# A transformer layer with pooling mixer, mLSTM and experts: column sums of the modulation by row products and a DRAM turn, router logits with the weights stationary, one channel order, output projection in one run

## The chip, the cores and the metric

The kernel runs on one core of a Trainium2 chip. The metric is the device time of one execution in microseconds (us). Before the change three runs gave 1613.83, 1614.59 and 1615.7 us; the median is 1614.59 us. The engines are TensorE (PE, with its weight loads shown apart as PEld), VectorE (DVE), ScalarE (ACT), GpSimd (POOL) and SyncE (SP), which here issues nearly all loads from DRAM.

## The reference, cut to what matters

256 latent tokens and 256 context tokens, model width 2048, all float32, one layer.

```python
sh1, sc1, g1, sh2, sc2, g2 = split(silu(c) @ w_mod + b_mod, 6)       # w_mod (2048, 12288)
xn  = rmsnorm(x) * norm1_g * (1 + sc1) + sh1
u   = xn @ w_in                                                      # columns p | q | o | k | v | gates
h_m = bidirectional chunkwise mLSTM(q, k, v, gates), started from the context's k, v, gates
p   = pooling mixer(u_p);  m = head_norm(h_m) * sigmoid(u_o)
h   = x + g1 * (concat(p, m) @ w_out)                                # w_out (2048, 2048)
fn  = rmsnorm(h) * norm2_g * (1 + sc2) + sh2
logits = fn @ w_group (4 groups), fn @ w_router (32 experts)         # top-1 group, top-2 experts in it
y   = sum over chosen experts e of weight_e * ((silu(fn @ w1[e]) * (fn @ w3[e])) @ w2[e])
out = rmsnorm(h + g2 * y) * final_g                                  # w1, w3 (32, 2048, 512), w2 (32, 512, 2048)
```

## The kernel before

**Plan and stages.** The first part of the kernel (everything up to the router) follows one list of steps, `plan`, that is built at lines 164 to 256 and emitted in order at lines 1019 to 1021. Each engine executes its own instructions in the order in which they were emitted. The list has six stages: 0 to 2 work on the first 8 row blocks of `w_in` for k and v, stage 3 on the rest of k and v and all of q, stage 4 on o, p, the pooling mixer (`pool`, 16 steps) and the output projection's parts 0 and 1, stage 5 (after `join`) on part 2 and the routes. A main step of stage 3 to 5 is a group of 12 matmuls 128x512 (`mm3`: high and low halves of a float32 split, three products for each of four row blocks). Each block of weights is loaded by SP, split into `hi` on ACT (line 548) and `lo` on DVE (line 549), one job ahead of its matmuls. Other steps are spread evenly among the main ones by the weights of `weight`: `da`, `df`, and `side`.

**Modulation sums.** Channel 2 is the gate g1, 3 the shift, 4 the scale, 5 the gate g2. For each of the four, 16 steps `da` each load one [128, 2048] slice of `w_mod` (1 MB) and add it, times a column of silu(c), into a tile (`do_da`, line 513, DVE). The sum over the 128 partitions is then made by `do_df` (line 515) in four steps per channel. Channels 2 and 5 need it as a row on all partitions: one matmul 128x512 with ones. Channels 3 and 4 need it as columns: eight matmuls per step with one moving column each (line 522 in the order 128j+p, line 523 in the order 16p+j), into `A2`, `B2` for the router and `A2p`, `B2p` for the experts.

**The mLSTM** is a generator (`mlstm`, line 710): each `side` step emits it up to its next `yield`. Its PE work is small; each of its steps waits for ACT or DVE work of the step before. In stage 4 there are 50 places for such steps.

**Output projection.** `do_out` (line 650): part 0 covers the pooling half (k0 = 0, 4), part 1 and part 2 the two halves of the mLSTM half (k0 = 8; k0 = 12), for four column blocks cb and two token tiles tt. Parts 0 and 1 add their product, times g1, into the residual with one DVE and one POOL operation each; part 2 with two DVE operations, and an ACT square for the norm.

**Router.** `do_route` (line 970) transposes a column block of h, copies it to SBUF, and multiplies: tokens stationary (128x128), router weights moving (36 columns), summed over 16 blocks in two PSUM tiles. `do_c0` (line 995) makes the constant part of the logits from `B2` with 16 matmuls. After the plan the logits are scaled (line 1032), the experts are chosen, and the experts' loop (line 1174) runs over 8 groups of four experts: gather, h1 and h3, y, scatter.

**Loads and slots.** All loads of this first part and of the experts stand in one list `stream`, in order of use. SP issues them in that order; each goes into one of 23 slots of 1 MB that the split halves and the mLSTM's tensors share, and waits until the slot's last reader is done. The experts' 1 MB loads of `w1` and `w3` (line 297) take four of each partition's 16 rows: 8 KB per partition, 32 KB apart in DRAM.

Of the kernel before, what the change touches and what calls it, by code (L numbers as in the profile page):

```python
# [9 lines left out]
F32 = mybir.dt.float32  # L10
# [3 lines left out]
OP = mybir.AluOpType  # L14
# [68 lines left out]
def hymba_kernel(ctx: ExitStack, tc: tile.TileContext, x, c, ctx_in, c_ctx, w_mod, b_mod, norm1_g, w_in,  # L83
# [66 lines left out]
    ORDER = (2, 4, 3, 5)  # L150
    DA_SHARE = {2: 2, 3: 36, 4: 22, 5: 16}
# [88 lines left out]
    i = plan.index(("out", 2, 3, 12, 1))  # L240
    plan[i:] = [o for o in plan[i:] if o[0] == "da"] + [plan[i], ("route", 2, 0), ("route", 2, 1), ("route", 3, 0), ("route", 3, 1)]
    plan.insert(plan.index(("in", "v", 0, 0, 1, 0)), ("late",))
    plan.insert(plan.index(("out", 1, 2, 8, 0)), ("wr",))
# [21 lines left out]
    for op in plan:  # L265
# [3 lines left out]
        elif op == ("out", 0, 0, 4, 1):  # L269
            for tt in range(2):  # L270
                add_load(("h", tt), x[128 * tt:128 * tt + 128, :])
        elif op == ("wr",):
            add_load("wr", (w_group[0].rearrange("(j p) f -> p j f", p=128),
                            w_router[0].rearrange("(j p) f -> p j f", p=128)))
# [13 lines left out]
        elif op[0] == "split":  # L288
            _, _, _, cb, k0 = op
# [18 lines left out]
    def ahead(upto):  # L308
        while issued[0] < min(len(stream), upto):
            key, src = stream[issued[0]]  # L310
            if key == "wr":
                t = slot([128, 2, KT, 36], name="wr")
                nc.sync.dma_start(t[:, 0, :, 0:4], src[0])
                nc.sync.dma_start(t[:, 0, :, 4:36], src[1])
# [76 lines left out]

    def do_late():
# [4 lines left out]
        nc.sync.dma_start(prm[0:16], norm2_g[0].rearrange("(j p) -> j p", p=128))  # L397
# [4 lines left out]
        nc.sync.dma_start(prm[80:112], b_mod[0, 3 * D:5 * D].rearrange("(j p) -> j p", p=128))  # L402
# [3 lines left out]
        nc.sync.dma_start(pj[:, 0, :], norm2_g[0].rearrange("(p k) -> p k", k=KT))  # L406
        nc.sync.dma_start(pj[:, 1:3, :], b_mod[0, 3 * D:5 * D].rearrange("(c p k) -> p c k", p=128, k=KT))
# [3 lines left out]
    def do_late2():  # L411
        p = ps(name="pcol")
        pe.transpose(p[:, 0:112], prms[0][0:112], ident[0:112, 0:112])
        act.activation(pcol, p[:, 0:112], AF.Copy)
# [6 lines left out]
    A2p = cst.tile([128, KT], F32, name="A2p")  # L421
    B2p = cst.tile([128, KT], F32, name="B2p")
# [92 lines left out]
    def do_df(ch, n):  # L515

        a = open_da[ch] if n < 3 else open_da.pop(ch)
        if ch in (3, 4):
            js = slice(4 * n, 4 * n + 4)
            o = ps(name="adac")  # L520
            for j in range(4 * n, 4 * n + 4):
                mm(o[:, j:j + 1], a[:, 128 * j:128 * j + 128], one, True, True)
                mm(o[:, KT + j:KT + j + 1], a[:, j:D:KT], one, True, True)
            oj, op_ = o[:, js], o[:, KT + js.start:KT + js.stop]
            bj = pcol[:, 80 + 16 * (ch - 3) + 4 * n:84 + 16 * (ch - 3) + 4 * n]
            if ch == 3:
                dve.tensor_tensor(B2[:, js], oj, bj, op=OP.add)
                dve.tensor_tensor(B2p[:, js], op_, pj[:, 1, js], op=OP.add)
            else:
                dve.scalar_tensor_tensor(A2[:, js], oj, 1.0, bj, op0=OP.add, op1=OP.add)  # L530
                dve.tensor_tensor(A2[:, js], A2[:, js], pcol[:, 4 * n:4 * n + 4], op=OP.mult)
# [800 lines left out]
```

## Time and profile before

| | |
|---|---|
| runs | 1613.83, 1614.59, 1615.7 us |
| profiled execution | 1616.64 us, span 1614.9 us |
| PE busy | 1381.3 us (86%) |
| DVE busy | 574.8 us (36%) |
| ACT busy | 268.9 us (17%) |
| POOL busy | 69.4 us (4%) |
| read from HBM | 571.5 MB, 355 GB/s over the span |
| chain that ended last | PE 43%, DMA 42%, issue 7%, DVE 6% |

The page cuts the span into 40 slices of about 40 us. Its shares of busy time are means over two very different parts: up to about 615 us the layer up to the router, then the experts. A busy PE is no proof of a PE at its peak: ends of matmuls are modelled, and the granted clock (1.0 is 2.4 GHz, 0.5 is 1.2 GHz) differs between stretches.

### The profile page before, as it was taken

Reading aid. Unit: us, or ns where it says so; the run is one execution under the profiler, and the core shown is the slowest. Engines: PE = TensorE matmul, PEld = TensorE weight load, DVE = VectorE, ACT = ScalarE, POOL = GpSimd, SP = SyncE. Lnnn points to the kernel's source line nnn. Section 1 sums busy time; section 2 is a strip of 40 time slices with the busy share of each in tenths; the row PEclk is TensorE's granted clock in tenths of the full one; section 3 lists DMA queues with packets and bytes.
Section 4 is the critical chain, followed back from the end, with each engine's and each line's share of the span. In section 5 each row is a group of like instructions: output and inputs, shape, how many; then the busy total and the mean of one; then the engine's idle time right before and its main releaser. Section 6 shows DMA issues by size and latency. Waiting matters only on the chain.

```text
span 1614.9 us, 16367 instructions
## 1 busy us (share of the span) xinstructions
PE 1381.3 (86%) x6697; PEld 765.1 (47%) x6697; DVE 574.8 (36%) x822; ACT 268.9 (17%) x406; POOL 69.4 (4%) x66
## 2 busy tenths in 40 slices
PE   5999999899999998799679679678689688688685
PEld 3566687688888787453142142142142142142122
DVE  3454779966677868412011011011011011011013
ACT  4322223532545312110010010010010010010011
POOL 0121100000000440000000000000000000000000
PEclk9999999999999988799899899899889889989898
DMA  8977986944559779999999999999999999999993
GB/s 276 346 270 266 371 311 227 371 157 156 208 193 347 230 311 419 406 421 422 423 422 422 422 422 422 422 423 422 422 422 423 422 422 422 423 422 422 422 388 117
DMA packets 138359, 574.73 MB, mean 356 GB/s; under 512 B 20248, under 2 KB 34152, under 8 KB 82088
## 3 DMA queue, kind: packets, MB, share of 16 engines
q1 hardware_dynamic: 133384, 572.28, 89.1%
q10 hardware_dynamic: 4704, 1.07, 0.3%
q8 instruction: 54, 0.88, 0.2%
q0 software_dynamic: 192, 0.29, 0.1%
q14 instruction: 25, 0.20, 0.0%
HBM read 571.50 MB, written 2.10 MB: 355 GB/s over the span
## 4 chain that ended last, share of the span: by engine, by line
PE 43%; DMA 42%; issue 7%; DVE 6%; POOL 1%; SPq 1%; ACT 1%; DVEq 0%; POOLq 0%; ACTq 0%
DMA raw<-in_w_dram 40%; PE po L123 8%; PE yp L123 7%; PE pg L123 5%; PE h L123 3%; PE pk L123 3%; PE pv L123 3%; PE pp L123 2%; PE pq L123 2%; PE adac L123 1%; POOL xT L489 1%; DMA raw<-in_w_mod_dram 1%; DVE da L513 1%; PE pc L123 1%; PE sc L123 1%
## 5 line engine op out<-in xcount | busy, mean ns | idle before, releaser
L123 PE MATMUL h<-raw,xg 128*32 128x512 f32 x2048 | 371.2, 694 | 147.7 <-DMA raw<-in_w_dram 147.6
L123 PEld LDWEIGHTS h<-raw,xg 128*32 128x32 f32 x2048 | 83.3, 124 | 430.5 <-DMA raw<-in_w_dram 271.1
L123 PE MATMUL yp<-raw,heT 128*32 128x512 f32 (+2 forms) x1056 | 215.2, 584 | 0.0
L1193 DVE TENSOR_TENSOR he<-he,h 128x512 f32<-128x512 f32 x8 | 5.5, 687 | 495.8 <-PE h L123 495.8
L549 DVE TENSOR_TENSOR lo<-raw,hi 128x2048 fp32r<-128x2048 f32 (+2 forms) x60 | 132.1, 2205 | 16.8 <-ACT hi L548 11.1
L123 PEld LDWEIGHTS yp<-raw,heT 128*32 128x32 f32 x1056 | 64.4, 110 | 145.3 <-issue 142.5
L123 PE MATMUL pg<-oh,raw 128*128 128x128 f32 x512 | 115.1, 394 | 12.1 <-DVE oh L1085 10.7
L548 ACT ACTIVATE hi<-raw 128x2048 fp32r<-128x2048 f32 (+2 forms) x60 | 107.5, 1797 | 107.1 <-PE po L123 35.2
L123 PEld LDWEIGHTS pg<-oh,raw 128*128 128x128 f32 x512 | 112.8, 312 | 17.2 <-DVE oh L1085 10.5
L1192 ACT ACTIVATE he<-h 128x512 f32<-128x512 f32 x8 | 4.8, 597 | 631.7 <-PE h L123 631.7
L1208 DVE TENSOR_TENSOR ye<-yp,gb 128x512 f32<-128x512 f32 (+2 forms) x33 | 20.8, 669 | 186.2 <-PE yp L123 186.2
L513 DVE SCALAR_TENSOR_TENSOR gb<-raw,sc,gb 128x2048 f32<-128x2048 f32 x32 | 75.5, 2360 | 0.1
L513 DVE SCALAR_TENSOR_TENSOR da<-raw,sc,da 128x2048 f32<-128x2048 f32 x30 | 72.3, 2411 | 4.3 <-DMA raw<-in_w_mod_dram 4.1
L1098 DVE TENSOR_SCALAR xg<-pg,A2p,B2p 128x128 f32<-128x128 f32 x64 | 24.9, 409 | 114.7 <-ACT xg L1100 114.7
L123 PE MATMUL sc<-ye,cT 128*128 128x512 f32 (+2 forms) x132 | 58.1, 589 | 3.5 <-DVE ye L1208 3.5
L123 PE MATMUL pk<-hi,xh 128*128 128x512 f32 x128 | 53.1, 415 | 2.4 <-DVE xh L492 2.4
L123 PE MATMUL pv<-hi,xh 128*128 128x512 f32 x128 | 53.3, 420 | 0.0
L123 PE MATMUL pk<-lo,xh 128*128 128x512 f32 x128 | 50.8, 397 | 2.1 <-DVE lo L549 2.1
L123 PE MATMUL pv<-lo,xh 128*128 128x512 f32 x128 | 51.4, 402 | 0.0
L123 PE MATMUL pv<-hi,xl 128*128 128x512 f32 x128 | 51.0, 398 | 0.0
L123 PE MATMUL pk<-hi,xl 128*128 128x512 f32 x128 | 50.9, 398 | 0.0
L1100 ACT ACTIVATE xg<-pg,B2p,A2p 128x128 f32<-128x128 f32 x64 | 27.0, 457 | 124.6 <-PE pg L123 116.2
(334 smaller groups left out, 1616.4 us busy)
## 6 DMA issues: line engine op xcount, KB each, us to landing
raw<-in_w_dram SPq DMA_DIRECT2D x380, 1024.0 KB, 19.8
raw<-in_w_mod_dram SPq DMA_DIRECT2D x90, 1024.0 KB, 7.2
raw<-in_w_in_dram SPq DMA_DIRECT2D x36, 1024.0 KB, 7.1
raw<-in_w_out_dram SPq DMA_DIRECT2D x16, 1024.0 KB, 6.1
raw<-in_w_mod_dram SPq DMA_DIRECT2D x8, 768.0 KB
raw<-in_w_in_dram SPq DMA_DIRECT2D x4, 768.0 KB
raw<-in_w_dram SPq DMA_DIRECT2D x4, 768.0 KB
x<-in_x_dram SPq DMA_DIRECT2D x2, 1024.0 KB
```

The source lines that it names most:

```text
L123: pe.matmul(out_, lhsT, rhs, start=start, stop=stop, **kw)
L489: nc.gpsimd.tensor_scalar(v, v, a_, b_, op0=OP.mult, op1=OP.add)
L513: dve.scalar_tensor_tensor(a, w, sc1[:, k:k + 1], a, op0=OP.mult, op1=OP.add)
L548: act.activation(hi, raw, AF.Copy)
L549: dve.tensor_tensor(lo, raw, hi.bitcast(F32), op=OP.subtract)
L1098: dve.tensor_scalar(xg[:, j, :], src, A2p[:, j:j + 1], B2p[:, j:j + 1], op0=OP.mult, op1=OP.add)
L1100: act.activation(xg[:, j, :], src, AF.Identity, scale=A2p[:, j:j + 1], bias=B2p[:, j:j + 1])
L1192: act.activation(he, h1, AF.Silu)
L1193: dve.tensor_tensor(he, he, h3, op=OP.mult)
L1208: dve.tensor_tensor(ye, yp, gbc_t[5][:, cs], op=OP.mult)
```

## The change

The modulation's channels come in the order 4, 3, 2, 5, with other shares per stage. For channels 3 and 4, `do_df` acts once per channel: four matmuls with 32 columns of ones stationary put the sums into four rows groups of one PSUM tile, ACT copies it, a POOL DMA writes four rows to DRAM, a second POOL DMA reads them back as [128, 16], and DVE adds the bias. There is one order of channels, 512c + 4p + u, for the router and the experts, so `A2p` and `B2p` go, and loads of router weights, norm weights and biases, the transposes, the gather and the experts' `w1` and `w3` follow it: those loads now read 1 MB without gaps. The output projection is one PSUM run over k0 = 0, 4, 8, 12 for each column block, wholly after `join`. Logits are computed with the router weights stationary, in two halves of a PSUM tile that a last matmul per token tile adds and turns. `do_c0` multiplies and sums on DVE and uses one matmul.

```diff
-    ORDER = (2, 4, 3, 5)
-    DA_SHARE = {2: 2, 3: 36, 4: 22, 5: 16}
+    ORDER = (4, 3, 2, 5)
+    DA_SHARE = {2: 8, 3: 28, 4: 26, 5: 14}
...
-    OUT_K = ((0, 4), (8,), (12,))
-    outs = [[("out", part, cb, k0) for cb in range(4) for k0 in OUT_K[part]] for part in range(3)]
-    stages += [run("o", 0) + run("p", 0) + [("pool",)] + outs[0] + outs[1]]
+    OUT_K = (0, 4, 8, 12)
+    stages += [run("o", 0) + run("p", 0) + [("pool",)]]
     last = [("join",)]
-    for job in outs[2]:
-        last.append(job)
-        if job[2]:
-            last.append(("route", job[2] - 1))
+    for cb in range(4):
+        for k0 in OUT_K:
+            last.append(("out", cb, k0))
+            if cb and k0 == 0:
+                last.append(("route", cb - 1))
...
-    plan[i:] = [o for o in plan[i:] if o[0] == "da"] + [plan[i], ("route", 2, 0), ("route", 2, 1), ("route", 3, 0), ("route", 3, 1)]
+    plan[i:] = [o for o in plan[i:] if o[0] == "da"] + [plan[i], ("route", 3, 0), ("route", 3, 1)]
...
-                             w[4 * g + e].rearrange("(p k) f -> p k f", k=KT)[:, 4 * jq:4 * jq + 4, :])
+                             w[4 * g + e].rearrange("(c p u) f -> p c u f", p=128, u=4)[:, jq])
...
-        nc.sync.dma_start(pj[:, 0, :], norm2_g[0].rearrange("(p k) -> p k", k=KT))
-        nc.sync.dma_start(pj[:, 1:3, :], b_mod[0, 3 * D:5 * D].rearrange("(c p k) -> p c k", p=128, k=KT))
+        for i, src in enumerate((norm2_g[0], b_mod[0, 3 * D:4 * D], b_mod[0, 4 * D:5 * D])):
+            nc.gpsimd.dma_start(pj[:, i, :].rearrange("p (c u) -> p c u", u=4), blocks(src))
...
         if ch in (3, 4):
-            js = slice(4 * n, 4 * n + 4)
+            if n < 3:
+                return
             o = ps(name="adac")
-            for j in range(4 * n, 4 * n + 4):
-                mm(o[:, j:j + 1], a[:, 128 * j:128 * j + 128], one, True, True)
-                mm(o[:, KT + j:KT + j + 1], a[:, j:D:KT], one, True, True)
...
+            for q in range(4):
+                mm(o[32 * q:32 * q + 32, :], ones[:, 0:32], a[:, 512 * q:512 * q + 512], True, True)
+            row = small([128, 512], "parts")
+            act.activation(row, o, AF.Copy)
+            dr = drow.tile([4, 512], F32, name=f"mod{ch}")
+            nc.gpsimd.dma_start(dr, row[0:128:32, :])
+            dst = B2 if ch == 3 else A2
+            nc.gpsimd.dma_start(dst.rearrange("p (c u) -> p c u", u=4), dr.rearrange("c (p u) -> p c u", u=4))
+            dve.tensor_tensor(dst, dst, pj[:, ch - 2, :], op=OP.add)
...
-            pe.transpose(p[:, 128 * u:128 * u + 128], hb[tt][:, 128 * j:128 * j + 128], ident)
+            pe.transpose(p[:, 128 * u:128 * u + 128], hb[tt][:, blk(4 * cb + u)], ident)
...
-            mm(lg[tt][:, 0:36], f[:, 128 * u:128 * u + 128], wr_t[0][:, 1, j, :], j == 0, j == KT - 1)
+            j, r = 4 * cb + u, 64 * (u % 2)
+            mm(lg[tt][r:r + 36, 0:128], wr_t[0][:, 1, j, :], f[:, 128 * u:128 * u + 128], j < 2, j >= KT - 2)
...
-        for j in range(KT):
-            mm(c0[:, 0:36], B2[:, j:j + 1].to_broadcast([128, 128]), wr[:, 0, j, :], j == 0, j == KT - 1)
+        dve.tensor_tensor(wr[:, 0], wr[:, 0], B2[:, :, None].to_broadcast([128, KT, 36]), op=OP.mult)
+        cs_ = small([128, 64], "fm_s")
+        dve.tensor_reduce(cs_[:, 0:36], wr[:, 0].rearrange("p j f -> p f j"), axis=mybir.AxisListType.X, op=OP.add)
+        mm(c0[:, 0:36], ones, cs_[:, 0:36], True, True)
...
-        dve.scalar_tensor_tensor(L[:, tt, :], lg[tt][:, 0:36], rstd2[:, tt:tt + 1], rbc, op0=OP.mult, op1=OP.add)
+        act.activation(lsum[0:36, tt], lg[tt][0:36, 0:128], AF.Copy)
+        dve.tensor_copy(lsum[64:100, tt], lg[tt][64:100, 0:128])
+        p = ps(name="lgt")
+        mm(p[:, 0:36], lsum[:, tt], two, True, True)
+        dve.scalar_tensor_tensor(L[:, tt, :], p[:, 0:36], rstd2[:, tt:tt + 1], rbc, op0=OP.mult, op1=OP.add)
```

## Rows read from the trace of the kernel before

**Rows 1.** The page, part 2: busy tenths and GB/s in 40 slices.

```profile
PE   5999999899999998799679679678689688688685
...
GB/s 276 346 270 266 371 311 227 371 157 156 208 193 347 230 311 419 406 421 422 423 422 422 422 422 422 422 423 422 422 422 423 422 422 422 423 422 422 422 388 117
```

**Rows 2.** Stretches: PE, PEld, DVE, ACT, POOL busy us; PEclk, DMA share, GB/s.

```profile
760.00:1541.00 781.00, 619.54 (x3051) 225.06 (x3050) 80.76 (x157) 27.78 (x61) 0.52 (x1) 0.92 1.01 422
```

**Rows 3.** The same view for stretches between 260 and 664 us.

```profile
260.00:337.00 77.00, 67.87 (x297) 53.72 (x296) 73.52 (x79) 32.86 (x35) 0.00 (x0) 0.93 0.83 310
337.00:514.00 177.00, 176.42 (x810) 149.26 (x809) 115.42 (x189) 76.74 (x121) 0.54 (x1) 0.96 0.57 201
...
597.00:635.00 38.00, 35.53 (x173) 30.13 (x173) 29.93 (x23) 8.20 (x17) 0.00 (x0) 0.83 1.02 419
635.00:664.00 29.00, 16.79 (x78) 14.40 (x80) 26.04 (x74) 5.59 (x15) 0.00 (x0) 0.60 1.01 421
```

**Rows 4.** PE waits from 337 to 640 us: total us, times, longest.

```profile
PE po L123 <- DVE lo L549: 2.5, 1, 2.5
```

**Rows 5.** The loads' queue (SP) from 596 to 640 us: start, us, instruction.

```profile
596.34 16.23 SPq L317 DMA_DIRECT2D raw<-in_w_mod_dram  x8
615.10 24.09 SPq L317 DMA_DIRECT2D raw<-in_w_dram  x12
```

**Rows 6.** The chain that ended last, in order of time: start, us, what.

```profile
340.68 2.77 PE po L123 x12
343.45 2.50 PE adac L123 x16
346.45 4.35 PE po L123 x12
...
596.31 10.05 PE po L123 x36
```

**Rows 7.** Stretches of two column-sum steps: the sums, then the matmuls behind.

```profile
343.50:345.90 2.40, 2.40 (x16) 2.40 (x16) 0.30 (x1) 1.65 (x4) 0.00 (x0) 1.00 0.00 0
346.50:350.80 4.30, 4.30 (x15) 3.36 (x13) 3.70 (x6) 0.47 (x1) 0.00 (x0) 0.60 0.21 48
```

**Rows 8.** The chain from 560 us on, around the last output groups.

```profile
615.51 7.84 PE po L123 x24
623.35 3.49 PE c L123 x32
...
632.44 2.65 PE po L123 x11
...
653.21 0.43 DVE L L1032 x2
...
663.91 7.32 PE h L123 x64
```

**Rows 9.** Groups by line and shape: busy us, mean ns, idle before.

```profile
L549 DVE TENSOR_TENSOR lo<-raw,hi 128x2048 fp32r<-128x2048 f32 x52 | 122.4, 2357 | 15.8 <-ACT hi L548 10.1 <-PE po L123 4.1 <-PE pp L123 1.5
...
L123 PEld LDWEIGHTS pg<-oh,raw 128*128 128x128 f32 x512 | 112.8, 312 | 17.2 <-DVE oh L1085 10.5 <-issue 6.7
...
L513 DVE SCALAR_TENSOR_TENSOR gb<-raw,sc,gb 128x2048 f32<-128x2048 f32 x32 | 75.5, 2360 | 0.1
...
L974 PEld LDWEIGHTS ht<-ca,raw 128*128 128x128 f32 x32 | 5.3, 193 | 2.2 <-issue 1.9
...
L893 ACT ACT_TABLE_LOAD x3 | 3.8, 1283 | 0.1
...
L990 DVE TENSOR_TENSOR wr<-wr,A 128x576 f32<-128x576 f32 x1 | 2.1, 2144 | 0.0
...
L939 ACT ACTIVATE oacc<-oacc 128x2048 f32<-128x2048 f32 x1 | 1.9, 1920 | 0.0
```

**Rows 10.** DMA issues: queue, count, KB each, median us to landing.

```profile
ut<-in_const_a_dram POOLq DMA_DIRECT2D x1, 64.0 KB, 6.1
...
gb<-in_b_mod_dram POOLq DMA_DIRECT2D x2, 8.0 KB, 4.3
```

More of the change, by code (lines that the diff above doesn't have):

```diff
@@ L239, in hymba_kernel @@
     assert not da
-    i = plan.index(("out", 2, 3, 12, 1))
-    plan[i:] = [o for o in plan[i:] if o[0] == "da"] + [plan[i], ("route", 2, 0), ("route", 2, 1), ("route", 3, 0), ("route", 3, 1)]
+    i = plan.index(("out", 3, 12, 1))
+    plan[i:] = [o for o in plan[i:] if o[0] == "da"] + [plan[i], ("route", 3, 0), ("route", 3, 1)]
     plan.insert(plan.index(("in", "v", 0, 0, 1, 0)), ("late",))
-    plan.insert(plan.index(("out", 1, 2, 8, 0)), ("wr",))
+    plan.insert(plan.index(("join", 0)), ("wr",))
     plan.insert(plan.index(("in", "k", 1, 1, 3, 0)), ("late2",))
@@ L268, in hymba_kernel @@
             add_load("wp", w_pool[0].rearrange("g (k p) f -> p (g k) f", p=128))
-        elif op == ("out", 0, 0, 4, 1):
+        elif op == ("out", 0, 4, 1):
             for tt in range(2):
@@ L288, in hymba_kernel @@
         elif op[0] == "split":
-            _, _, _, cb, k0 = op
+            _, _, cb, k0 = op
             r0 = 128 * k0
@@ L312, in ahead @@
                 t = slot([128, 2, KT, 36], name="wr")
-                nc.sync.dma_start(t[:, 0, :, 0:4], src[0])
-                nc.sync.dma_start(t[:, 0, :, 4:36], src[1])
+                v = t[:, 0].rearrange("p (c u) f -> p c u f", u=4)
+                for c in range(4):
+                    nc.sync.dma_start(v[:, c, :, 0:4], src[0][:, c])
+                    nc.sync.dma_start(v[:, c, :, 4:36], src[1][:, c])
             else:
@@ L390, in hymba_kernel, with blocks, blk @@
     prms = []
+    def blocks(row):
+        return row.rearrange("(c p u) -> p c u", p=128, u=4)
+    def blk(j):
+        return slice(512 * (j // 4) + j % 4, 512 * (j // 4) + 512, 4)
     def do_late():
@@ L648, in hymba_kernel, with do_out @@
     sq = cst.tile([128, 2, 4], F32, name="sq")
-    def do_out(part, cb, k0, gi):
-        key = "out", part, cb, k0
-        if part == 1:
-            while 1 not in cat_done and next(side, 0) is None:
-                pass
+    def do_out(cb, k0, gi):
+        key = "out", cb, k0
         hi, lo = parts_of[key]
@@ L657, in do_out @@
         tt = gi
-        first, last = k0 == OUT_K[part][0], k0 == OUT_K[part][-1]
+        first, last = k0 == OUT_K[0], k0 == OUT_K[-1]
         if first:
@@ L674, in do_out @@
             h = hb[tt][:, cs]
-            if part < 2:
-                dve.tensor_tensor(t, p, gbc_t[2][:, cs], op=OP.mult)
-                nc.gpsimd.tensor_tensor(h, h, t, op=OP.add)
-                return
             n = 256 if (cb, tt) == (3, 1) else 512
@@ L968, in hymba_kernel @@
     rbc = cst.tile([128, 36], F32, name="rbc")
+    lsum = cst.tile([128, 2, 128], F32, name="lsum")
+    two = cst.tile([128, 36], F32, name="two")
     def do_route(cb, tt):
@@ L992, in do_join @@
         lg.extend((ps(name="lg0"), ps(name="lg1")))
+        nc.gpsimd.memset(lsum, 0.0)
+        nc.gpsimd.memset(two, 0.0)
+        nc.gpsimd.tensor_copy(two[0:64, 0:36], ident[0:64, 0:36])
+        nc.gpsimd.tensor_copy(two[64:128, 0:36], ident[64:128, 64:100])
         act.activation(scr[:, 1:2], one, AF.Sqrt)
```

41 lines of the change are left out of this document (14 added, 27 removed).

## The prediction, made before the result was known

> **What bounds the kernel now.** I read first the page's slices, then the stretches, then the waits, the chain and the loads' queue of the place where the two parts meet. The slices show two regimes [rows 1]: up to slice 15 PE is busy at 90% or more nearly everywhere while the loads run at 150 to 370 GB/s; from there to the end the loads run at 421 to 423 GB/s and PE is only partly busy. The stretch of the experts says the same: DMA share 1.01 at 422 GB/s, PE 619.5 of 781 us [rows 2]. So in the second part only one thing counts: when the uninterrupted stream of expert loads starts. The queue shows it: the last eight w_mod loads go out from 596.34, the first expert load at 615.10 us [rows 5]. From there to the end of the profiled execution (1616.64 us) lie 1001.5 us, which I take as fixed: the bytes are the same.
>
> The start is set by the first part, which is PE's: from 337 to 514 us PE is busy 176.4 of 177 us with DVE at 115.4 [rows 3], and PE's largest wait for DVE from 337 to 640 us is 2.5 us [rows 4]. From 260 to 337 us it is DVE's: 73.5 of 77 us, PE loses 9.1 [rows 3]. SP issues ahead of PE as far as slots come free: 615.10 is 20 us before the last output matmul (632.44 + 2.65 = 635.1) [rows 5, 8]. So the forecast is a balance of PE time up to that matmul, and then of how far ahead of it the stream starts.
>
> **The column sums removed.** Eight steps (channels 3 and 4, four each) of 2.50 us go [rows 6]: -20.0. Behind each the array runs slower: with only one-column matmuls in it the granted clock of the step is still 1.00, of the 4.3 us behind it 0.60, that is mostly the 1.2 GHz level [rows 7]; 12 matmuls took 4.35 instead of 2.77, 36 took 10.05 instead of 8.31 [rows 6]. At 1.6 for each of the eight: -12.8. Together **-32.8** (ends -20 and -34).
>
> **Row products added.** Four 32-column matmuls are eight instructions; 64 of that shape take 7.32 us [rows 8], so 0.9 per channel: **+1.8**. The ACT copy is off PE's path.
>
> **The turn through DRAM, channel 3.** DVE's add waits for the ACT copy (0.6, a quarter of DVE's 2.36 us for four times the columns [rows 9]) and two POOL DMAs one after the other. The nearest rows land in 4.3 and 6.1 us [rows 10], so 9.2 to 12.8 us. DVE is in order: behind the add are the weights of the first mLSTM head, directly followed by the matmuls that need them (no filler stands between these two `side` steps in the new list), two `da` and a `lo`. PE has about one group (2.8 us) of work before it needs DVE. I take **+8** (0 if the wait is covered, 13 at most). The Trainium skill (DMA: Bandwidth & Descriptors, Anatomy of one DMA) gives a fixed cost near 2.0 us per DMA; by it the turn would be an estimated 5 us, this term 2 and that of channel 4 about 1, and the sum 10 less; the trace's small POOL loads are twice that, beside other traffic.
>
> **The mLSTM stretch gets denser.** Before, 24 groups of the output projection and the 32 of o and p stood ahead of `join`, and 50 places for mLSTM steps were spread over them. Now o, p and pooling are all the filler, and by the steps' order the mLSTM's part ends after 28 groups. PE's own work in it: 177 us less 32 groups (89), four sum steps with their slow stretch (16) and pooling (16 steps at a third of a group, 15) leaves 57 for the mLSTM; with 28 groups (78) that is 135 us. DVE's: of its 115.4 us [rows 3], 15 `lo` and 11 `da` at 2.36 [rows 9] are 61, the rest 54, some 6 of it pooling. In the new stretch there are 14 `lo` and 16 `da` (71), so 119, and with the turn's idle 9 it is 128 of 135. The two nearest rows: DVE at 65% and PE loses 0.6 of 177; DVE at 95% and PE loses 9.1 of 77, which on 135 us is 16. By single steps: after o's last group the sigmoid (1.92) and two table loads (1.28 each) [rows 9] lie ahead of the second head's exponentials with no filler, some 4; the second direction's state product follows its DVE weighting at once, 2; the two normalisations reach PE through 12 to 14 us of DVE work (three `da` or `lo`, 7.1, and an estimated 5 to 7 of small operations) with three groups, 8.3 us, of filler, 4 and 6; two heads without filler, 2 together. I take **+18** (0.6 to 30).
>
> **The turn of channel 4** falls just ahead of 260 us, where DVE is full; nine idle microseconds of DVE there come out late, less what the somewhat later `da` steps give back: **+5** (0 to 11). Six more `da` loads go to stage 2, whose slices run at 266 to 371 GB/s of 422 [rows 1]; they and the POOL issues of `pj` are hidden; if not, 3.
>
> **c0.** 3.49 us of PE go [rows 8]. But its one matmul now waits for DVE, which has queued since the column block's end two adds on 512 columns (1.2), `lo`, `da`, `lo` (7.1), the product (2.14) [rows 9] and a sum (0.6 to 2.1), 12 us, while PE has two groups (5.5). Stall 6, net **+3** (-3 to +5).
>
> **Routes.** Route 2 moves ahead of the last output matmul. A pair costs 5.6 us (626.84 to 632.44) and slows the next two groups by 2.3 (7.84 against 5.54) [rows 8]: **+8** (5.6 to 8). Its transposes now read every fourth element. The gather's loads of strided columns take 312 ns against 193 for the unstrided transpose [rows 9]; eight per pair, three pairs: 0 to 2.9, I take **+2**. The Trainium skill (SBUF — State Buffer, Door 1) has 16-byte lines, so that a step of 4 floats would pay as one of 16 does; by it this is 2.9.
>
> **Sum.** -32.8 + 1.8 + 8 + 18 + 5 + 3 + 8 + 2 = +13: the last output matmul ends near 648. The start of the stream: 23 slots less nine tensors that live throughout (h, two gates, four halves of the mixer's output, router weights) and four in use leave ten; four are freed per job, so the last w_mod load waits for a slot freed by the job four jobs before the end: 8 groups (22.2) and a route pair (5.6) are 28 us before the last matmul, against 20 before. 648.1 - 27.8 = 620.3, **5.2 us later** than 615.1. The experts' first matmul needs no own term: after the last output matmul come some 4.8 us of adds, route 3 and the new turn of the logits, then the 10.7 us from 653.21 to 663.91 [rows 8], together 663.6, as before; DVE's backlog of 635 to 650 [rows 3] is gone, but the loads don't gain by that. POOL's adds and the 16 DVE adds of parts 0 and 1 were off the path. 1616.64 + 5.2 = 1621.8; the profiled execution lies 2.05 above the median of the runs, so **1620 us**.
>
> **The rivals.**
> 1. *PE's relief comes through.* If DVE keeps ahead and the turns are covered (the three terms of 31 become 8, as PE's 0.6 of 177 at full density speaks for), the last matmul ends at 625, the stream starts at 597, and the time is 1597. Against it: DVE at 93% in the dense stretch.
> 2. *The stream starts late* (the slower side's mechanism): slots of the `hi`/`lo` pairs aren't free as I count, so that the lead is 12 us and not 28; it decides below 23 us. Then it starts at 636: 1636. For it: SP waited for PE and DVE in all of the first part; the lead before was only 20 [rows 5, 8].
> 3. *Expert loads without gaps run faster.* For it nothing in the rows; against it the DMA share of 1.01 at 422 GB/s [rows 2]. 268 MB of w1 and w3 take 636 us; 3% is 19 us, hence 1601. The Trainium skill (DMA: Bandwidth & Descriptors, Where 436 GB/s comes from) puts the ceiling of the ports at 435 GB/s; by it 3% is all there could be.
>
> **Chances.** Forecast 0.54, own range 1611 to 1631; rival 1 0.27, rival 2 0.14, rival 3 0.05. About 0.2% (3.2 us) is what a measurement here can tell from no change. Faster: rivals 1 and 3, 0.32. Within: a quarter of the forecast's case, 0.14. Slower: the rest of it and rival 2, 0.54. Range: from rival 1 to just past rival 2, 1597 to 1638.
>
> **What would show it.** Right: no column sums of one column, granted clock near 1.0 between o's groups; DVE above 90% and PE losing 15 to 30 us between the first o group and the last mLSTM transposes; DVE waits of 8 us or more for POOL's DMAs, twice; a PE wait for c0's DVE sum of about 6; the first expert load near 620 and 28 us before the last output matmul; 422 GB/s afterwards. Wrong: PE without waits in the mLSTM stretch, a first expert load before 605 or after 635, or another rate of the expert loads.

## The result, and the profile after

The changed kernel takes 1588.04 us (median of 4 runs, 1586.01 to 1588.99) against 1614.30 for the kernel before in the same comparison: ratio 0.9828, 95% interval 0.9812 to 0.9844. The forecast was 1620, slower, with a range of 1597 to 1638; the time lies below the range. The profiled execution took 1588.16 us, its span is 1586.4 (before 1614.9). The 28.5 us of span stand in two places: the first expert load goes out 23.9 us earlier, and from there to the end it is 4.6 us shorter.

The page's PE, granted clock and GB/s of the changed kernel, 40 slices of 39.7 us; answers to [rows 1]:

```profile
PE   5999998999999998998698698698688688689686
...
PEclk9999899899999998999999899999899899899898
...
GB/s 279 343 293 285 375 286 220 238 297 160 291 247 351 317 308 422 421 423 421 422 422 422 422 422 422 422 422 421 422 422 422 421 422 422 422 422 423 422 385 111
```

The two regimes are still there, and slice 15 is at full rate from its beginning on: before it was at 419 and slice 16 at 406. The rate of the second part is what it was [rows 2]. A stretch inside it, columns as in rows 2:

```profile
700.00:1500.00 800.00, 648.25 (x3140) 238.52 (x3132) 88.14 (x168) 27.19 (x60) 0.51 (x1) 0.92 1.01 422
```

So expert loads without gaps don't run faster, and all depends on when their stream begins. The loads' queue of the changed kernel; answers to [rows 5]:

```profile
580.21 0.39 SPq L319 DMA_DIRECT2D raw<-in_w_out_dram  x1
585.39 0.82 SPq L319 DMA_DIRECT2D raw<-in_w_mod_dram  x2
591.24 8.99 SPq L319 DMA_DIRECT2D raw<-in_w_dram  x8
```

591.24 stands against 615.10. Two w_mod loads go out just ahead of it, where before there were eight, so the stream starts without that backlog; and before, the rate fell to 388 GB/s between 660 and 680, when the first expert products were late (first h at 663.9 [rows 8], now at 626.1). Both fit the 4.6 us behind the first load, which the prediction took as fixed; how much each makes was not measured.

Stretches of the changed kernel: the one that the prediction called dense (135 us from the first o matmul on), the same up to the first output matmul, the output projection, and the change to the experts; answers to [rows 3]:

```profile
344.00:479.00 135.00, 132.20 (x613) 108.99 (x612) 106.15 (x149) 66.20 (x104) 4.23 (x5) 0.99 0.62 226
...
344.00:511.00 167.00, 163.22 (x749) 133.73 (x747) 130.32 (x185) 78.02 (x125) 6.56 (x7) 0.99 0.68 248
511.00:600.00 89.00, 87.37 (x417) 68.99 (x416) 72.45 (x46) 35.36 (x34) 0.00 (x0) 1.00 0.87 324
...
600.00:620.00 20.00, 14.74 (x77) 11.18 (x75) 12.89 (x51) 4.57 (x13) 0.00 (x0) 0.90 1.01 423
```

DVE is at 106 of the 135 us and at 130 of the 167, not at 95%; PE loses 2.8 and 3.8. The granted clock of the output projection is 1.00, where before it was 0.83 from 597 to 635. PE's waits from 337 to 640 us (total, times, longest); answers to [rows 4]:

```profile
PE pos L123 <- DVE gw L1080: 3.9, 1, 3.9
PE intra L123 <- DVE w L897: 2.8, 1, 2.8
PE lg L123 <- ACT fT L978: 1.7, 4, 0.7
...
PE pp L123 <- DVE lo L556: 1.0, 1, 1.0
PE po L123 <- DVE lo L556: 0.6, 1, 0.6
```

The first of these comes behind the last output matmul. The rest are a few microseconds, where the prediction had some 30. No row waits for c0. The end of the output projection in the chain (start, us, what); answers to [rows 8]:

```profile
540.23 0.47 PE ht L975 x4
540.70 1.86 PE po L123 x8
542.56 0.56 PE lg L123 x8
543.12 0.68 PE ht L975 x4
543.80 0.93 PE po L123 x4
544.73 0.56 PE lg L123 x8
545.29 14.55 PE po L123 x62
559.85 0.14 PE c L123 x2
```

A route pair is 2.3 us of ht and lg here, with output matmuls in between, and the 62 matmuls behind it run at 0.235 us each (the next two pairs take 3.9 and 2.0 us). Before, the pair at 626.8 took 5.6 us, and the 24 matmuls behind the pair ahead of it 0.327 each. c0 takes 0.14 us in place of 3.49.

All kernels side by side, in order of the sections below. "Last out" is the end of the last output matmul; the first three columns of numbers are of the profiled execution, in us from the start of the span. The kernel before ran beside each of the others, with medians of 1614.3 to 1616.9; the ratios take that into account, differences of two medians do not.

| Kernel | last out | first expert load | span | median | ratio to before, 95% interval |
|---|---|---|---|---|---|
| before | 637.6 | 615.1 | 1614.9 | 1614.3 | |
| changed | 610.4 | 591.2 | 1586.4 | 1588.0 | 0.9828 (0.9812 to 0.9844) |
| e1b, sums by one column, two orders | 634.0 | 614.8 | 1609.9 | 1610.5 | 0.9967 (0.9951 to 0.9982) |
| e2, the same, one order | 621.6 | 602.5 | 1595.1 | 1596.8 | 0.9872 (0.9852 to 0.9893) |
| e13, sums alone | 614.1 | 592.4 | 1593.0 | 1594.4 | 0.9863 (0.9847 to 0.9880) |
| e3, old channel order | 609.9 | 590.8 | 1586.0 | 1587.9 | 0.9814 (0.9792 to 0.9836) |
| e5, output in three parts | 611.8 | 592.4 | 1589.7 | 1592.0 | 0.9849 (0.9833 to 0.9866) |
| e4, old logits | 614.7 | 595.0 | 1589.3 | 1590.0 | 0.9832 (0.9815 to 0.9849) |
| e10, old c0 | 612.7 | 593.6 | 1590.0 | 1589.1 | 0.9830 (0.9814 to 0.9847) |
| e9, shares 2, 34, 26, 14 | 599.0 | 579.9 | 1575.9 | 1578.8 | 0.9770 (0.9754 to 0.9787) |
| e8, shares 8, 28, 30, 10 | 607.0 | 576.1 | 1577.5 | 1579.4 | 0.9770 (0.9750 to 0.9791) |
| e12, shares 8, 28, 34, 6 | 612.3 | 576.7 | 1580.0 | 1585.9 | 0.9827 (0.9804 to 0.9851) |
| e11, shares 2, 34, 30, 10 | 595.4 | 564.6 | 1564.9 | 1567.4 | 0.9700 (0.9684 to 0.9717) |
| e7, adds later in the list | 612.2 | 593.1 | 1587.1 | 1588.5 | 0.9823 (0.9803 to 0.9842) |
| e14, adds on POOL | 602.9 | 583.8 | 1578.7 | 1585.4 | 0.9812 (0.9786 to 0.9838) |
| e15, e14 with e11's shares | 593.0 | 562.2 | 1562.2 | 1563.8 | 0.9665 (0.9647 to 0.9684) |

### The profile page after: what moved, and what is told of

It reads as the page before. It is cut to its first block, busy times and chain, and to the rows that moved or that the text cites. A ratio compares the mean times of both kernels' runs of the same rounds, so it can differ in the third digit from the quotient of the medians.

```text
span 1586.4 us, 16019 instructions
## 1 busy us (share of the span) xinstructions
PE 1358.3 (86%) x6559; PEld 731.3 (46%) x6559; DVE 555.8 (35%) x790; ACT 268.2 (17%) x410; POOL 41.4 (3%) x61
## 4 chain that ended last, share of the span: by engine, by line
DMA 59%; PE 27%; issue 6%; DVE 4%; POOL 1%; ACT 1%; SPq 1%; DVEq 0%; ACTq 0%; POOLq 0%
DMA raw<-in_w_dram 57%; PE po L123 7%; PE pk L123 4%; PE pv L123 3%; PE yp L123 2%; PE pp L123 2%; DVE lo L556 1%; POOL xT L497 1%; PE pq L123 1%; PE ada L123 1%; PE inter L123 1%; PE pc L123 1%; PE pd L123 1%; DMA x<-in_ctx_dram 1%; PE intra L123 1%
## 5 line engine op out<-in xcount | busy, mean ns | idle before, releaser
L123 PE MATMUL pg<-oh,raw 128*128 128x128 f32 x512 | 123.1, 409 | 12.1 <-DVE oh L1096 10.7
L556 DVE TENSOR_TENSOR lo<-raw,hi 128x2048 fp32r<-128x2048 f32 (+2 forms) x60 | 128.8, 2147 | 5.8 <-ACT hi L555 5.7
L123 PEld LDWEIGHTS pg<-oh,raw 128*128 128x128 f32 x512 | 120.8, 330 | 17.2 <-DVE oh L1096 10.5
L1109 DVE TENSOR_SCALAR xg<-pg,A,B 128x128 f32<-128x128 f32 x64 | 25.0, 410 | 122.2 <-ACT xg L1111 122.2
L1111 ACT ACTIVATE xg<-pg,B,A 128x128 f32<-128x128 f32 x64 | 27.0, 457 | 132.3 <-PE pg L123 128.9
## 6 DMA issues: line engine op xcount, KB each, us to landing
raw<-in_w_dram SPq DMA_DIRECT2D x4, 768.0 KB, 12.4
```

The costliest lines, as they stand in the source:

```text
L123: pe.matmul(out_, lhsT, rhs, start=start, stop=stop, **kw)
L556: dve.tensor_tensor(lo, raw, hi.bitcast(F32), op=OP.subtract)
L1109: dve.tensor_scalar(xg[:, j, :], src, A2[:, j:j + 1], B2[:, j:j + 1], op0=OP.mult, op1=OP.add)
L1111: act.activation(xg[:, j, :], src, AF.Identity, scale=A2[:, j:j + 1], bias=B2[:, j:j + 1])
```

## The experiments

Theory T1: the gain is the column sums, 2.5 us a step and the slow clock behind them, and it reaches the start of the expert stream. Rivals: T2, the output projection in one PSUM run and the shorter end of DVE's work; T3, the expert loads without gaps. Every edit is to the changed kernel unless said otherwise.

**e1b and e2: the one-column sums put back.** e1b has both matmuls; the sums in the second order go where nothing reads them. e2 has the first matmul of the two alone. Neither has a turn through DRAM. (A first form of e1b, with a tile of its own for the second order, needs more SBUF than is left, and has no time.)

```diff
-            for q in range(4):
-                mm(o[32 * q:32 * q + 32, :], ones[:, 0:32], a[:, 512 * q:512 * q + 512], True, True)
...
+            for j in range(4 * n, 4 * n + 4):
+                mm(o[:, j:j + 1], a[:, blk(j)], one, True, True)
+                mm(o[:, KT + j:KT + j + 1], a[:, 128 * j:128 * j + 128], one, True, True)
```

> The changed kernel with channels 3 and 4 summed by one-column matmuls again: four steps per channel, 8 one-column matmuls each, in both channel orders as before (the second order is written where nothing reads it); no row products, no turn through DRAM. T1 (the gain is the sums' 2.5 us per step and the slow clock behind them, passed on to the start of the expert stream): the first expert load goes out 15 to 30 us later than 591 and the time is 15 to 30 us above the changed kernel's (eight steps at 2.5 and 1.6 us, less what DVE's wait for the turn had cost); granted clock near 0.6 behind each step. T2 (gain from the output projection's order): already down to some 4 us, so within 5 us of the changed kernel.

> As the run with one-column sums in both orders, but in one channel order only: 4 one-column matmuls per step instead of 8, so the matmuls' own time is halved and the eight steps and the slow stretch behind each stay. T1, if the slow stretch behind a step costs its 1.6 us whatever the step's length: some 10 us less than with both orders (eight times 1.25), so 8 to 20 above the changed kernel. T1, if the slow stretch goes with the length of the step: half of that run's excess, with a granted clock behind the steps nearer to 1.0.

e1b gives back 22.5 of the 26.3 us (1610.5 against 1588.0), and its first expert load goes out at 614.84, as before. e2 gives back 8.7. Why it is less than half shows in the chain. e1b, from 240 us (start, us, what):

```profile
240.15 2.52 PE adac L123 x16
242.67 7.25 PE pv L123 x24
249.92 2.52 PE adac L123 x16
252.44 7.26 PE pv L123 x24
```

and e2 at the same place:

```profile
242.24 1.64 PE adac L123 x8
243.87 5.67 PE pv L123 x24
249.55 1.64 PE adac L123 x8
251.18 5.71 PE pv L123 x24
```

24 matmuls behind a step of 16 instructions (8 one-column matmuls) take 7.25 us, behind one of 8 they take 5.67. The granted clock of the two stretches, first e1b, then e2 (columns as in rows 2):

```profile
242.67:249.92 7.25, 7.25 (x26) 5.81 (x26) 3.95 (x6) 0.72 (x3) 0.00 (x0) 0.76 0.30 97
```

```profile
243.87:249.55 5.68, 5.68 (x27) 4.66 (x26) 3.76 (x4) 0.71 (x3) 0.00 (x0) 1.00 0.14 27
```

So behind 2.5 us of one-column matmuls PE runs for a while at the lower of its two levels, and behind 1.6 us of them, here, it does not: the slow stretch does not come with every step. Not every step of e1b had one either; the third in the chain is followed by 12 matmuls in 2.88. The kernel before had one step without it too: 24 matmuls in 5.68.

```profile
578.68 2.50 PE adac L123 x16
581.18 5.68 PE po L123 x24
```

e2 saves 0.88 us in each of eight steps, 7.0. In e1b's chain the matmuls behind five of the steps take 7.8 us more than the same ones in e2 (7.25, 7.26, 5.26, 3.96 and 3.29 us against 5.67, 5.71, 3.58, 2.44 and 1.83). Together that is 14.8; between the last output matmuls of the two lie 12.4, so e2 loses a little elsewhere.

**e13: the sums alone.** The kernel before with the row products and the turn, and the one channel order that they need; output projection, plan, logits and c0 as before.

> One part of the change alone: the kernel before with the column sums of channels 3 and 4 by row products and the turn through DRAM, and the one channel order that this needs; the output projection in three parts, w_mod's old order and shares, logits and c0 stay as before. T1 (the sums are the gain, and the other parts about cancel): 20 to 26 us below the kernel before, first expert load near 592, no granted clock of 0.6 between o's groups. If the gain is spread over the parts: 10 to 18 us below. By the prediction's terms (33 saved, 2 for the row products, 13 for the two turns): 18 below.

22.2 us faster than before (ratio 0.9863, 0.9847 to 0.9880). T1 holds from this side too. Between the first o matmul and the first output matmul before took 172.3 us (337.3 to 509.6), e13 157.1 (337.3 to 494.4): four of the eight steps lie there, and four at 2.5 + 1.6 give 16.4, less 0.9 for row products 15.5. Further on some of it is lost again: from 511 to 600 PE is busy 77.8 of 89 us in e13, with these waits (337 to 640 us):

```profile
PE ht L982 <- DVE raw L690: 7.3, 3, 4.7
PE lg L123 <- ACT fT L985: 5.0, 4, 3.2
...
PE lg L123 <- DVE fT L987: 4.4, 1, 4.4
```

All three are the routes, which wait for a column block of h that DVE completes late (it is busy 75.0 of the 89 us), with three parts to add. In the whole change the adds of two parts are gone, and these waits shrink to 1.7 us (lg for fT); and from first load to end e13 takes 1000.6 us where the changed kernel takes 995.2.

**e3 and e5: the rivals.** e3 puts back channel order 16p+j with its 32 KB strides. In it a route's channels lie all along a row of h, and three of the four routes come before the output projection has been added to the later column blocks; so the logits are others and the tokens go to other experts. The work is of the same kind.

```diff
-        return slice(512 * (j // 4) + j % 4, 512 * (j // 4) + 512, 4)
+        return slice(j, D, KT)
...
-                             w[4 * g + e].rearrange("(c p u) f -> p c u f", p=128, u=4)[:, jq])
+                             w[4 * g + e].rearrange("(p k) f -> p k f", k=KT)[:, 4 * jq:4 * jq + 4, :])
```

> The changed kernel with one channel order still, but the old one: channel 16p+j, so that each expert load reads pieces of 8 KB that lie 32 KB apart, and the turn is read back in pieces of 64 bytes. T1: within 4 us of the changed kernel, expert loads at 421 to 423 GB/s. T3 (loads without gaps are the gain): some 20 to 26 us slower, with the expert loads below 415 GB/s.

1587.9 against 1588.0: T3 falls. Its stretch from 700 to 1500 us runs at 422 GB/s, as the changed kernel's.

e5 puts back the three parts, with w_mod's old order and shares (stages 2 to 5: 2, 36, 22, 16).

```diff
-    ORDER = (4, 3, 2, 5)
-    DA_SHARE = {2: 8, 3: 28, 4: 26, 5: 14}
+    ORDER = (2, 4, 3, 5)
+    DA_SHARE = {2: 2, 3: 36, 4: 22, 5: 16}
...
-    OUT_K = (0, 4, 8, 12)
+    OUT_K = ((0, 4), (8,), (12,))
...
```

> The changed kernel with the output projection in three parts again (k 0 and 4, k 8, k 12, each with its own eviction and its adds on DVE and POOL), with the old order of w_mod's stages and their shares; sums by row products, logits and channel order as changed. T1 (the sums): within 10 us of the changed kernel, still some 20 us below the kernel before. T2 (one PSUM run): 20 to 26 us slower than the changed kernel, the last routes behind DVE's backlog as before.

3.9 us slower than the changed kernel: by its time T2 is not the gain either. But this small number is the difference of two larger ones. From the first o matmul to the end of the last output matmul there are 300.3 us before, 276.8 in e13, 275.7 in e5 and 266.7 in the changed kernel. So the sums save 23.5 us there, new logits and c0 on top of them 1.1, and the output projection in one run, with the new order and shares, another 9.0. Ahead of o the changed kernel loses instead: o begins at 343.7, in e5 at 336.0, in the other two at 337.3. The experiments on w_mod's shares and on the turns show with what. T2 is a real part of the change, and a loss ahead of o hides most of it.

**e4 and e10: logits and c0.** e4:

```diff
-            mm(lg[tt][r:r + 36, 0:128], wr_t[0][:, 1, j, :], f[:, 128 * u:128 * u + 128], j < 2, j >= KT - 2)
+            mm(lg[tt][:, 0:36], f[:, 128 * u:128 * u + 128], wr_t[0][:, 1, j, :], j == 0, j == KT - 1)
...
```

> The changed kernel with the logits by the old product (tokens stationary, router weights moving, 36 columns each), so that the copies lsum and the second product lgt go; all else as changed. T1: the part between the first output matmul and the last is 3 to 10 us longer, since 64 products with 36 columns follow 64 loads of tokens instead of weights, less 2 to 3 us for the turn of the logits that goes; time +2 to +8 us. T2: 0 to +3. If the new way of routing is worth nothing by itself: within 2 us.

e10:

```diff
-        dve.tensor_tensor(wr[:, 0], wr[:, 0], B2[:, :, None].to_broadcast([128, KT, 36]), op=OP.mult)
...
-        dve.tensor_reduce(cs_[:, 0:36], wr[:, 0].rearrange("p j f -> p f j"), axis=mybir.AxisListType.X, op=OP.add)
-        mm(c0[:, 0:36], ones, cs_[:, 0:36], True, True)
+        for j in range(KT):
+            mm(c0[:, 0:36], B2[:, j:j + 1].to_broadcast([128, 128]), wr[:, 0, j, :], j == 0, j == KT - 1)
```

> The changed kernel with the bias part c0 by 16 matmuls again instead of DVE's product and sum with one matmul. If the new c0 makes PE wait for DVE (the prediction's 6 us, net 3 for the change): 0 to 3 us faster than the changed kernel. If its DVE work is done long ahead (it runs at 515.8, some 70 us before it is needed) and PE's 3.5 us are on the path: first expert load 3 to 4 us later, time +2 to +4.

The times, 2.0 and 1.1 us above the changed kernel, are not told apart from no change by their intervals. In the profiled executions, each the slowest of its four, the last output matmul ends 4.3 and 2.3 us later, the first expert load goes out 3.8 and 2.4 later. Of e10's 2.3 us, 1.4 lie ahead of o, where its edit changes nothing. Such scatter is common: in the six kernels that are alike up to o (the changed one, e3, e4, e8, e10, e12), o begins at 340.6 to 345.1. In these executions neither part of the change makes PE wait, and both save PE time: 4.3 and 0.9 us from o on.

**e9, e8, e11, e12: how w_mod's steps are shared out.** One line each:

```diff
-    DA_SHARE = {2: 8, 3: 28, 4: 26, 5: 14}
+    DA_SHARE = {2: 2, 3: 34, 4: 26, 5: 14}
```

> The changed kernel with six fewer of w_mod's steps in the third stage and six more in the fourth (shares 2, 34, 26, 14). The changed kernel begins the output columns o 6.4 us later than the kernel before (343.7 against 337.3). If the six w_mod loads and DVE adds that the change put into the third stage do that (the loads compete with those of w_in, PE waits 3.9 us for w_mod there): o begins near 338, the first expert load goes out near 586, time 4 to 6 us less. If it is DVE's total of work ahead of o, which stays the same: within 2 us.

9.2 us faster than the changed kernel. The prediction put six more w_mod steps in the third stage at nothing; they cost the change about as much as its output projection saves. The stretches from 150 us on, the changed kernel first, then e9:

```profile
150.00:160.00 10.00, 6.14 (x36) 3.06 (x38) 6.84 (x7) 0.00 (x0) 0.00 (x0) 0.93 0.94 350
160.00:170.00 10.00, 9.28 (x36) 5.11 (x29) 2.52 (x2) 0.60 (x1) 0.00 (x0) 0.56 1.04 405
```

```profile
150.00:160.00 10.00, 9.49 (x56) 5.34 (x54) 2.57 (x5) 0.60 (x1) 0.00 (x0) 1.00 0.93 332
160.00:170.00 10.00, 10.00 (x52) 6.92 (x52) 3.58 (x4) 1.92 (x1) 0.00 (x0) 1.00 1.04 395
```

In the changed kernel PE waits there for w_mod loads (3.9 us in two waits; e9 0.5), and the matmuls behind the wait run at a granted clock of 0.56: 36 in ten microseconds where e9 does 52. A wait is paid twice. All of this lies ahead of channel 4's turn, whose row products start at 254.2 us in the changed kernel. The last sums of the channels before it, first in the changed kernel, then in e5, which has two w_mod steps in the third stage as e9 has:

```profile
L123 PE MATMUL adac<-ca,parts x16: 251/312/374, 162.4 to 180.5; 128*128 128x2 f32 x16
```

```profile
L123 PE MATMUL adac<-ca,parts x16: 166/251/272, 156.4 to 171.7; 128*128 128x2 f32 x16
```

k, v and q take the same 960 matmuls in all kernels. The 601st of them starts at 240.2 us in the changed kernel, at 231.6 in e9 and at 230.9 before. So the six loads cost 8.6 us before the turn begins; o begins 10.2 us earlier in e9.

> The changed kernel with 10 instead of 14 rows of w_mod's last channel left for the last stage (4 more in the stage before). If the stream's start goes by when slots come free behind the jobs of the last stage, fewer loads ahead of the first expert load let it go out earlier: 4 groups of lead at most, first expert load near 580 to 585, time 5 to 10 us less, unless DVE's four more adds in the stage before cost PE waits there (up to 8 us back). If the start goes by the end of PE's work whatever the loads: within 3 us of the changed kernel.

8.6 us faster. The first expert load goes out 31 us before the last output matmul ends, in the changed kernel 19: with fewer w_mod loads in the last stage the expert loads get their slots sooner. Only part of it comes through, because the early loads still wait for slots (SP waits 18.4 us for output matmuls between 576 and 645, and the rate is 337 GB/s from 580 to 600): from first load to end it is 1001.4 us, not 995.2.

> The changed kernel with both shifts: shares 2, 34, 30, 10. If the gains of the shorter last stage (8.6 us measured) and of the emptier third stage (4 to 6 expected) add up: 12 to 15 us below the changed kernel, first expert load near 571. If stage five then is short of DVE (34 to 30 steps there): the 8.6 alone or less.

20.6 us faster; the two shifts (9.2 and 8.6) add up, and a little more.

> The changed kernel with 6 instead of 14 steps of w_mod left for the last stage, 8 more in the stage before (shares 8, 28, 34, 6). If the start of the expert stream goes on following the number of loads behind which it queues: first expert load near 562 and 12 to 17 us less than the changed kernel. If DVE is full in the stage before (it was at 82% there with 4 more steps): no better than the 8.6 us of the run with 10, or worse, with PE waits for DVE of 5 us and more between 344 and 511.

The outcome is that of the second case: 2.1 us, within the uncertainty of no change. From 344 to 511 us PE is busy 157.3 of 167, it loses 9.7 where the changed kernel loses 3.8. But DVE is not full: it is busy 139.1 us there, as in e11 (139.8), where PE loses 3.7. What differs is that DVE waits 6.4 us for channel 3's turn (2.8 in e11). Whether PE's waits come from that was not tried.

**e7, e14, e15: the turns through DRAM.** e7 puts DVE's adds behind the two turns into the step of the join, more than 100 steps later in the list.

> The changed kernel with DVE's adds of the biases behind the two turns through DRAM moved to the join, so that DVE never waits for a turn. If DVE's waits of 4.7 and 2.6 us for the turns stood on the path (as the prediction priced them, 5 and 8): 4 to 7 us faster than the changed kernel, first expert load near 585. If they are absorbed by what DVE has ready for PE: within 2 us.

1588.5, the same; but it does not answer the question, since DVE's instruction did not move. The add of channel 4 in e7 (instruction, count, durations, first and last start):

```profile
L989 DVE TENSOR_TENSOR A<-A,pj x1: 176/176/176, 267.5 to 267.5; 128x16 f32<-128x16 f32 x1
...
  DMA A<-mod: 5.0, 1
```

and in the changed kernel, with what DVE does behind it:

```profile
265.64 0.18 DVE L538 TENSOR_TENSOR A<-A,pj 128x16 f32<-128x16 f32 x1 [4.74 <-DMA A<-mod]
265.85 0.18 DVE L540 SCALAR_TENSOR_TENSOR A<-A,pj 128x16 f32<-128x16 f32 x1
265.94 2.34 DVE L521 SCALAR_TENSOR_TENSOR da<-raw,sc,da 128x2048 f32<-128x2048 f32 x1
268.32 0.69 DVE L734 SCALAR_TENSOR_TENSOR rows<-rows 64x512 f32<-64x512 f32 x1
```

DVE waits 4.7 us, and then come the gates' rows, for which PE waits. So the adds were given to POOL (for channel 4 as a product and an add):

```diff
-            dve.tensor_tensor(dst, dst, pj[:, ch - 2, :], op=OP.add)
+            nc.gpsimd.tensor_tensor(dst, dst, pj[:, ch - 2, :], op=OP.add)
```

> The changed kernel with the adds behind both turns done by POOL (the sum by an add, for channel 4 then a product and an add), so that DVE has no wait for a turn at all; they cannot move back to DVE's list as they did when they were only put later. If DVE's wait ahead of the gates' rows (4.7 us) delays PE: the wait of 4.1 us for the rows shrinks to about 2, as with one-column sums, the granted clock of 0.59 behind it goes, and the time falls by 3 to 6 us. If the turns are covered: within 2 us of the changed kernel, with the same PE wait for the rows.

In its profiled execution PE's wait for the rows is 1.9 us, not 4.1, and behind it the clock does not fall. The changed kernel first, then e14:

```profile
270.00:280.00 10.00, 5.64 (x23) 4.01 (x22) 9.55 (x31) 2.40 (x4) 0.00 (x0) 0.90 0.96 363
280.00:290.00 10.00, 10.00 (x30) 6.77 (x29) 6.98 (x10) 0.70 (x3) 0.00 (x0) 0.59 0.20 56
```

```profile
270.00:280.00 10.00, 7.64 (x33) 4.97 (x32) 9.49 (x32) 3.10 (x6) 0.00 (x0) 1.00 0.89 316
280.00:290.00 10.00, 10.00 (x48) 8.17 (x49) 8.87 (x12) 3.98 (x4) 0.00 (x0) 1.00 0.41 145
```

30 against 48 matmuls in 280 to 290; o begins at 337.9 and not at 343.7 (the kernels that are alike up to o had 340.6 to 345.1), and the first expert load goes out 7.5 us earlier. The times are not as clear: 1580.4 (the profiled one), 1582.9, 1587.9 and 1590.0, median 2.6 us below the changed kernel with overlapping intervals. Two of the four are at the changed kernel's time. Whether the clock falls behind the remaining wait in those was not seen; the scatter fits it but does not show it.

> The same with w_mod's shares 2, 34, 30, 10, which took 20.7 us off the changed kernel. If the gain of fewer steps in the third stage was the loads' and not the turn's, the adds on POOL give about as much here as in the run before (0 to 6 us below 1567). If the shift had already moved the gates' rows out of the turn's way: nothing here, and the run before gives 3 to 6.

1563.8, the fastest kernel of all, 3.6 us below e11; the two intervals just touch (0.9665, 0.9647 to 0.9684, against 0.9700, 0.9684 to 0.9717). It beats the changed kernel by 24 us and the kernel before by 3.3%.

Of e9's gain the six loads made most: 8.6 us stand before the turn. The turn's wait costs the changed kernel 5.8 us up to o in the profiled execution (e14), with e11's shares 3.0 (o at 333.1 in e11, 330.2 in e15). The two are not independent, since e9 also moves the turn's add (from 265.6 to 273.4) and has no PE wait for the rows.

## Why the prediction was wrong, step by step

The sum said that the last output matmul would end 13 us later; it ends 27.2 earlier. (The prediction had read its end before as 635.1, off the chain; the last row is at 637.24 + 0.40.)

| Step, as predicted (us) | Measured | By |
|---|---|---|
| column sums -32.8, row products +1.8: -31.0 | -31.1 in the profiled executions, -25.1 by the medians; with the turns' cost in it -23.6 | last out of e14 less that of e1b; that of the changed kernel less that of e1b |
| turn of channel 4, +5 | +5.8 in the profiled execution; both turns +2.6 by the times (unclear) | start of o in e14 |
| turn of channel 3, +8 | no PE wait; 1.7 at most | o to last out, 266.7 in the changed kernel, 265.0 in e14 |
| mLSTM stretch denser, +18 | 3.8 lost by PE, of which 2.8 in one wait | stretch 344 to 511 |
| six w_mod loads in the third stage, 0 (else 3) | +8.6 | the 601st matmul of k, v and q, e9 |
| adds of parts 0 and 1, "off the path", 0 | -9.0, together with the new order and later shares | o to last out, e5 |
| c0, +3 | -0.9 | o to last out, 266.7 and 267.6 in e10 |
| routes, +8; strided transposes, +2 | -4.3 with the new logits; +0.4 | e4; 207 against 193 ns for 32 loads |
| lead of the stream, 28 against 20 | 19.1 against 22.5 | the queue |
| from first load to end, unchanged | -4.6 | the queue |
| rate of the expert loads, unchanged | unchanged | e3 |

What was right. The column sums were priced well, with the slow clock as a part of it; that it agrees to 0.1 us is partly luck, since e14's profiled execution was its fastest, and before, the clock fell behind seven of the eight steps and not behind each. The rate of the second part was right too. The turn of channel 4 takes 10.3 us from the start of the ACT copy (255.34) to DVE's add (265.64), the prediction had 9.2 to 12.8; and it does reach PE. Of the single DMAs the two writes landed after 5.8 and 2.9 us, the two reads after 3.2 and 2.4; the prediction had 4.3 to 6.1 for each [rows 10]. The Trainium skill (DMA: Bandwidth & Descriptors, Anatomy of one DMA) gives about 2.0 us per DMA; the 2.4 of the one read is nearest to it, channel 4's write took nearly three times that.

**The step that failed** is the dense mLSTM stretch, with the two that rest on the same reasoning (turn of channel 3, c0): together +29, measured +5 at most (3.8, 1.7, -0.9). It took the DVE share of the new stretch (95%) and read off what PE would lose there from the only other stretch with such a share [rows 3]. Both halves failed. The share came out at 79% (106.2 us in 135; up to the first output matmul 130.3 in 167). And a share alone does not give the loss, as the kernels show for 344 to 511 us, which hold mostly the same work in each: DVE 106.9, 118.4, 130.3, 139.8 and 139.1 us of 167 (before, e13, changed, e11, e12), PE lost 0.2, 0.7, 3.8, 3.7 and 9.7. At the same share e11 loses 4 and e12 10. The row that it went by was read rightly: from 260 to 337 us before, PE lost 1.6 us to the gates' rows and the rest to two waits for `lo`, behind a DVE that had no gap from 304 to 333.

```profile
PE pq L123 <- DVE lo L549: 7.5, 2, 6.8
```

But one late `lo` made 6.8 of the 9.1 us, and that does not scale to another stretch by its share. Of the single stalls that the prediction listed, the one behind the sigmoid and the table loads came (2.8 us, it had 4); the normalisations (10), the state product (2) and the heads (2) show no wait.

Beneath that lies an assumption, which the text ahead of the prediction states as a fact: that each engine runs its instructions in the order in which the list emits them. The traces refute it. c0's product runs here, long before its matmul at 559.85 and behind nothing of what the prediction queued ahead of it:

```profile
L1003 DVE TENSOR_TENSOR wr<-wr,B x1: 752/752/752, 515.8 to 515.8; 128x576 f32<-128x576 f32 x1
```

The matmuls of the routes stand between output matmuls (540.23 to 545.29 above), and the add of channel 4 that e7 moved by 215 steps stays at 267 us (that of channel 3, moved by 113, at 396 against 394). The order in which the engines run is another than that of the list, which still shapes it (e5, e9), but not step by step. All the prediction's stalls "with no filler" were read from a list that the engines don't follow step by step. The routes' +8 fell with it, since it took pairs that stand together (5.6 us, with slow matmuls behind); here they cost 2.0 to 3.9 and the clock stays at 1.00.

The second failure is of the other sign: six w_mod loads in the third stage, "hidden; if not, 3". Hidden they were not: with the slow clock behind the waits they cost 8.6 us. Had this been seen and the rest left as it was, the forecast would have been still slower. The third is a term put at nothing without a row: the adds of parts 0 and 1 were taken to be off the path. Once the sums are gone, routes wait for them (e13: 7.3 and 4.4 us for DVE), and without them the stretch from o on is 9.0 us shorter. The lead of the stream was mis-sized, 28 us for 19.1. With the output projection in one run it follows the number of w_mod loads in the last stage (19 us with 14, 31 with 10, 36 with 6); no row of before, with its 16 loads and 22.5 us, could show that. The table's rows differ from their forecasts by 38 us in all, of the 40 between forecast and measurement, though they are not independent of each other.

By the prediction's own list, "PE without waits in the mLSTM stretch, a first expert load before 605" was what would show it wrong. Rival 1, relief comes through (first load 597, 1597 us), was the right mechanism with 0.27; it was 9 us short. It still had costs for routes (10) and c0 (3), nothing for the adds that go and a fixed end; its lead of 28 us and the six loads at nothing went the other way, so that the nearness is in part luck.

## What to carry to other kernels

Price the matmuls that go, with the slow matmuls behind them, from rows; but before pricing a wait in the new list, see in a trace whether the engines follow the list at all: one instruction far from its place settles it. Loads put into a stage are hidden only if the trace of the new kernel shows no wait for them, and a short PE wait can cost again in the clock behind it. A small difference between two kernels can hide two large ones: compare them stretch by stretch, at the same instruction. When a change pays less than its removed work, vary how the moved loads are shared out: here that one line was worth 20.6 us more.

## What the runs showed of the hardware that was not expected

Behind a step of 2.5 us with one-column matmuls the granted clock of the following 7.25 us was 0.76 (partly the 1.2 GHz level), behind one of 1.6 us it stayed at 1.00 (2.4 GHz). It did not fall behind each step of 2.5 us (578.68 before). The same fall stands behind plain waits: 0.56 from 160 to 170 us after a stretch with PE busy 6.1 of 10, 0.59 from 280 to 290 after 5.6 of 10. In e14 it was 1.00 after 7.6 of 10, in e8 0.55 (160 to 170) after 7.45 of 10.

Loads of stationary columns every fourth element (16 bytes) took 330 ns in the gather where every sixteenth had taken 312 [rows 9], and 207 in ht where adjacent ones had taken 193. So the 2.9 us that a deduction from the Trainium skill (SBUF — State Buffer, Door 1: lines of 16 bytes) gave for ht was not seen; for the gather the shorter step is indeed no cheaper.

One and the same product on DVE (router weights times A, 128x576, fp32) took 2144 ns before, 1256 in e13 and 749 in the changed kernel. Before, POOL was adding at the same time (567.88 to 570.39, the product from 568.9 on); in e13 it was adding too (from 551.05 on, the product at 552.9), in the changed kernel it was idle. Whether that is the cause was not tried, and it does not tell the first two apart.
